# A two-layer decoder trunk: bias tables, value weights, score maxima and output splits moved in the order of work

## The chip, the cores and the metric

The kernel runs on one core of one Trainium2 chip. The metric is device time in microseconds for one execution of the whole program, the median of several runs. Five engines work side by side: TensorE (PE, with its weight loads shown as PEld), VectorE (DVE), ScalarE (ACT), GpSimd (POOL) and SyncE (SP), which here issues all transfers.

## The reference

Two decoder layers act on x of 512 rows by 1024 columns, in fp32. Each layer is: half-step SwiGLU feed-forward, token mixer, half-step SwiGLU feed-forward. Each of these six sub-layers is wrapped in the same way:

```
hn = rmsnorm(x, pre_g) * (1 + scale) + shift
y  = rmsnorm(fn(hn), post_g)
x  = x + res_w * gate * y          # shift, scale, gate from silu(c) @ w_mod + b_mod
ffn(h) = (silu(h @ w_gate) * (h @ w_up)) @ w_down            # inner width 2816
```

The mixer of layer 0 is latent attention with 16 heads. The mixer of layer 1, the one that the change touches, is dilated sliding-window attention with 16 heads of width 64 and three groups of dilation 1, 4 and 16:

```
proj = (h @ w_in)                  # per group g: queries, keys, values, 16 heads x 64
s    = q k^T / 8 + bias[bucket(rel * dilation)]    # -inf outside the window
lse  = logsumexp(s);  p = exp(s - lse);  o_g = p v
alpha = softmax over the three groups of lse
out  = (sum_g alpha_g o_g) @ w_o
```

The bias is a table of 32 buckets by 48 (16 heads for each of 3 groups), looked up by the bucketed distance. Since the groups are joined by a softmax over their log-sums, the kernel uses one maximum and one denominator over all three groups for each row and head.

## The kernel before

**Products.** Every fp32 weight tile is split into a high and a low half (`weights`, lines 128 to 136): a transfer into a "raw" buffer (5 of them), a copy on ScalarE that rounds to the high half (line 133), and two subtractions on VectorE, 512 columns each, for the low half (line 135). High and low halves live in rings of `SLOTS` = 6. A product is then three matrix multiplications, high by high, high by low and low by high (`mm3`, lines 148, 149 and 150). One projection tile is 8 such triples, 24 matrix multiplications of 128 by 512. Results go to PSUM banks under two tags, "mm" and "aux", with 4 banks each. SBUF tiles of 512 columns come from one pool of 44 slices; short-lived ones from small pools under the tags "silu", "gg" (2 buffers each), "sq" and "u" (4 each).

**Between sub-layers.** `transition` (line 478) finishes one sub-layer and starts the next: for each of four row blocks, the last products of the old one (`tail`), the norm and residual, transposes and modulation into the new h; after the second row block it calls the next sub-layer's `prepare`, and then its "heads", for the dilated layer six projection tiles of head pair 0, once for each half of the rows. Nothing here has an order written by hand: the planner orders by program order as priority and by its own idea of readiness.

**The dilated layer** (`Dil`, `rest` from line 1400). Heads are handled in 8 pairs. In `rest` the gates are fetched, the bias tables are made (`tables`: three one-hot tables of 33 by 384 and the bias table are loaded, three small products go to PSUM on line 989, are copied out and written to memory as `tv`), the bias tiles of pair 0 are read back from `tv` with a shifting row offset (`bias_of`, 12 transfers for a pair, line 1005), and then a loop with an order written by hand for TensorE, ScalarE and VectorE begins. In that loop, pair p attends while the projection tiles of pair p + 1 fill TensorE, six tiles (`ORDER`, slots n = 0 to 5), and for p = 0 and p = 4 twelve value tiles more (`value_tile`), which make the values of four or three pairs at once, group by group, four tiles each. SyncE and GpSimd are not part of the order by hand.

**A pair's start.** Slot n = 0 holds: transposes of the previous pair's group-0 probabilities on TensorE (`turn_up`, line 1244, two steps), their copies out of PSUM on VectorE (`turn_down`, line 1256), the scores of group 0 (`scores` 0 and 1, line 1118, two "mm" banks each), whose bias addition and row maximum is one VectorE instruction (line 1135), and the 32 by 32 transposes of group 2 on VectorE (line 1258). The projection tile of the slot follows. Slot 1 has the weighted sums of the previous pair (`weigh`, line 1277) and the scores of groups 1 and 2.

**Weights ahead.** `ahead` starts weight loads up to a given count beyond the tile at work. In the loop it keeps 5 tiles ahead; in the value tiles, up to 6, and in the last tile of each group of four one more load after each of the four pairs of row blocks (line 1345).

**The end of the layer.** After seven rounds the three value tiles of pair 7 are made (`LAST`); each tile's transposes to row order (line 1093) run behind the next tile, and the last one's as `later()`. Then each earlier pair's output is split into high and low (`put_o`, lines 711 and 712), the last pair's maxima go through memory to be joined across groups (`tops`), its exponentials follow (line 1194) and its denominators go through memory as well (`norm`, `norm_out`). Under a second order by hand, now for TensorE and VectorE alone, `part` n makes the output projection over the first `PART` = 3 pairs, eight parts, mixed with the last pair's turns and weighted sums. The other five pairs' products come in `tail`, in the next transition.

Of the kernel before, what the change touches and what calls it, by code (L numbers as in the profile page):

```python
# [22 lines left out]
PART = 3  # L23
# [3 lines left out]
SLOTS = 6  # L27
KQ = 2
UB = 4
SB = 4  # L30
# [506 lines left out]
class Ffn:  # L537
# [17 lines left out]
    def prepare(self):  # L555
        self.gate_up_load(0, True)
# [34 lines left out]
    def head(self, ft, lo, hi):  # L591
        banks = [self.t.bank()[:, : hi - lo] for g in range(2)]
        self.gate_up_mm(ft, lo, hi, banks, range(KT))
        self.gate_up_out(ft, lo, hi, banks)
# [371 lines left out]
class Dil(Mixer):  # L966
# [9 lines left out]
        (2, tuple((j, j * P, P, 384) for j in range(4))),  # L976
    )

    def tables(self):
        t, nc = self.t, self.t.nc  # L980
        self.tv = t.dram.tile([3, 16, 384], F32, name="tv")
        hot = [t.s() for _ in range(3)]
        tab = t.t("u", UB)
        nc.sync.dma_start(tab[0:32, 0:48], t.a["rel_bias"])
        nc.vector.memset(tab[32:33, 0:48], 1.0)
        for g in range(3):
            nc.sync.dma_start(hot[g][0:33, 0:384], t.a["dil_hot"][g])
            b = t.bank("aux")
            nc.tensor.matmul(
                b[0:16, 0:384], tab[0:33, 16 * g : 16 * g + 16], hot[g][0:33, 0:384], start=True, stop=True  # L990
            )
            v = t.t("gg")
            nc.vector.tensor_copy(v[0:16, 0:384], b[0:16, 0:384])
            nc.sync.dma_start(self.tv[g], v[0:16, 0:384])

# [47 lines left out]
    def head(self, u, lo, hi):  # L1043
        if lo == 0 and u == 0:
            self.qkv = {}
            self.pairs = {}
            self.later = None
        self.tile(0, self.ORDER[u], lo, hi)

    def prepare(self):  # L1050
        t = self.t
        self.wt = {(0, u): t.weights_sliced(t.a["dil_in"][0, u]) for u in self.ORDER[:2]}

    def tile(self, p, u, lo, hi):
        t, nc = self.t, self.t.nc
        g, kind = divmod(u, 3)
        n = hi - lo
        if lo == 0:
            if (p, u) not in self.wt:
                self.wt[p, u] = t.weights(t.a["dil_in"][p, u])  # L1060
            self.qkv[p, u] = t.s()
        w = self.wt[p, u]
        b = t.bank()[:, :n]
        for k in range(KT):
            t.mm3(b, [x[:, k, :] for x in w], [x[k][:, lo:hi] for x in t.h], k == 0, k == KT - 1)
        dst = self.qkv[p, u]
        runs = (SEQ, P, 32)[g]
        part = runs * n // SEQ
        at = runs * lo // SEQ
        if kind == 1:  # L1070
            at = runs - at - part
        for q in range(1 if g < 2 else 4):
            if g == 0:
                out, src = dst[:, at : at + part], b
            elif g == 1:
                out = dst.rearrange("p (r l) -> p r l", r=4)[:, :, at : at + part]
                src = self.order(b, 1)
            else:
                out = self.split(dst, 2)[:, q, :, at : at + part]
                src = self.order(b, 2)[:, q]  # L1080
            if kind == 1:
                src = self.back(src)
            nc.scalar.activation(out, src, AF.Copy)  # L1083
        turn, self.later = self.later, None
        if turn:
            turn()
        if kind == 2:

            def turn():
                x = t.bank("aux")  # L1090
                for j in range(4):
                    r = slice(j * P, (j + 1) * P)
                    nc.tensor.transpose(x[:, r], dst[:, r], t.ident)
                v = self.qkv[p, u] = t.s()
                nc.vector.tensor_copy(v, x)

            self.later = turn
# [232 lines left out]
    def value_tile(self, p, g, j):  # L1330

        t, nc = self.t, self.t.nc
        n = (self.BLOCKS_V[p][1] - p) * P
        if (g, j) == (0, 0):
            self.made = []
        if j == 0:
            wide = [t.wide() for _ in range(2)] if g < 2 else []
            halves = [x[:, d * SEQ : (d + 1) * SEQ] for x in wide for d in range(2)]
            self.made.append(halves or [t.s() for _ in range(4)])
        b = t.bank()[:, :n]  # L1340
        for k in range(KT):
            w = [x[:, k % 2 * n :][:, :n] for x in self.wt[p, g, k // 2]]
            h = [self.keys_of(x[k], g, j) for x in t.h]
            t.mm3(b, h, w, k == 0, k == KT - 1)
            if j == 3 and k % 2:
                self.ahead(self.at + SLOTS + k // 2 + 1)
        dst = self.made[g][j][:, :n]
        out = t.s()[:, :n] if g == 2 else dst
        nc.scalar.activation(out, b, AF.Copy)
        if g == 2:  # L1350
            for a in range(4):
                nc.sync.dma_start(
                    dst[32 * a : 32 * a + 32], out.rearrange("(l a) v -> a l v", a=4)[a]
                )
        if (g, j) == (2, 3):
            self.v = self.made

    def slot(self, p, n):

        if n == 0:  # L1360
            if p:
                up = [self.turn_up(p - 1, step) for step in range(2)]
                for step in range(2):
                    self.turn_down(p - 1, step, up[step])
            self.scores(p, 0)
            self.scores(p, 1)
            if p:
                self.turn(p - 1, 3)
        elif n == 1:
            if p == 7:  # L1370
                self.scores(p, 2)
                self.scores(p, 3, "aux")
            if p:
                for step in range(4):
                    self.weigh(p - 1, step)
            if p < 7:
                self.scores(p, 2)
                self.scores(p, 3, "aux")
        elif n == 4:
            self.biases(p + 1)  # L1380
        elif n == 5:
            self.turn(p, 2)
# [17 lines left out]
    def rest(self):  # L1400
        t = self.t
        t.gates(self)
        self.of = []
        self.bias = {}
        self.tables()
        self.biases(0)
        self.coming, self.loaded, self.at = self.loads(), 0, 0
        with t.tc.manual_schedule(engines={PE, ACT, DVE}):
            for p in range(7):
                values = [(p, g, j) for g in range(3) for j in range(4) if p in self.BLOCKS_V]  # L1410
                for n, at in enumerate([(p + 1, u) for u in self.ORDER] + values):
                    self.slot(p, n)
                    self.ahead(self.at + min(SLOTS - 1 + max(n - 6, 0) % 4, SLOTS))
                    self.beside(p, n)
                    if n < 6:
                        self.tile(*at, 0, SEQ)
                    else:
                        self.value_tile(*at)
                    self.behind(p, n)
                    if n < 6 or n % 4 == 1:  # L1420
                        self.at += 1 if n < 6 else 4
            for n, u in enumerate(self.LAST):
                self.slot(7, n)
                self.ahead(self.at + SLOTS - 1)
                self.beside(7, n)
                self.tile(7, u, 0, SEQ)
                self.at += 1
        self.later()
        for x in self.of[:PART]:
            self.put_o(x)  # L1430
        t.new_y()
        self.tops(self.pairs[7])
        for x in self.of[PART:]:
            self.put_o(x)
        for i in range(TT):
            t.unpark(i)
        self.exps(7, (2, 0, 1, 3))
        self.norm(self.pairs[7])
        order = (2, 0, 1, 3)
        with t.tc.manual_schedule(engines={PE, DVE}):  # L1440
            for n in range(6):
                self.part(n)
            for n, step in enumerate(order):
                self.turn(7, step)
                if n:
                    self.weigh(7, order[n - 1], order[0], order[-1])
                if n in (0, 1):
                    self.part(6 + n)
            self.norm_out(self.pairs[7])
            self.weigh(7, order[-1], order[0], order[-1])  # L1450
            self.finish(7)
        self.put_o(self.of[-1])
# [118 lines left out]
```

## Time and profile before

| | |
|---|---|
| median of 3 runs | 2277.46 us (2275.86 to 2278.70) |
| the profiled execution | 2277.86 us, span 2276.0 us |
| mean granted TensorE clock | 0.995 |
| TensorE busy | 2236.2 us, 98% |
| weight loads busy | 1879.6 us, 83% |
| VectorE busy | 1184.7 us, 52% |
| ScalarE busy | 849.8 us, 37% |
| GpSimd busy | 105.0 us, 5% |
| read from HBM | 281.76 MB, 126 GB/s over the span |

Reading: a timeline row gives start, duration, engine, line, operation, output and inputs, how many instructions were merged, and in square brackets the idle time of that engine before the row and what ended it. A row of a stage table gives the stretch, its length, for each of PE, PEld, DVE, ACT and POOL the busy time and the count, then the granted TensorE clock, the share of the transfer engines in use and the GB/s. A row of a group gives the line, engine, operation, tiles, shape, count, then busy time and mean ns of one, then idle time ahead of them and what ended most of it.

### The profile page before, as it was taken

What the parts mean: (1) busy time and instruction counts of PE and PEld (TensorE: products, weight loads), DVE (VectorE), ACT (ScalarE), POOL (GpSimd) and SP (SyncE); (2) the same over time, 40 slices, a digit from 0 to 9 for tenths busy, and PEclk for the clock granted to TensorE, in tenths of its full rate; (3) what the DMA queues carried; (4) which work ended last, traced back from release to release, by engine and by line L of the source; (5) the groups of instructions that cost most, each with busy time, mean ns of one, the idle gap of its engine ahead of it and who ended that gap; (6) DMA issues with size and microseconds to landing.
All of it is one profiled execution on the core that took longest, in us unless ns stands there. A gap on an engine that the chain in (4) does not pass through costs nothing.

```text
span 2276.0 us, 30275 instructions
## 1 busy us (share of the span) xinstructions
PE 2236.2 (98%) x11410; PEld 1879.6 (83%) x11410; DVE 1184.7 (52%) x2697; ACT 849.8 (37%) x1737; POOL 105.0 (5%) x143
## 2 busy tenths in 40 slices
PE   7999999999999999999999999999999999999998
PEld 5888888877888888898888887988898878888887
DVE  7666566577755456464555463234423457233344
ACT  4422235577623222353222353334342535332222
POOL 0000001210110000020000010000000002000000
PEclk9999999999999999999999999999999999999999
DMA  8575662211255365245544433433333442233231
GB/s 307 166 241 185 185 231 72 96 56 48 91 159 176 107 200 184 93 140 135 188 167 146 123 124 90 118 85 96 79 96 97 93 119 78 74 121 102 84 111 38
DMA packets 124344, 290.07 MB, mean 127 GB/s; under 512 B 44818, under 2 KB 49701, under 8 KB 124198
## 3 DMA queue, kind: packets, MB, share of 16 engines
q1 hardware_dynamic: 124198, 288.15, 41.1%
q8 instruction: 89, 1.46, 0.3%
q14 instruction: 57, 0.47, 0.1%
HBM read 281.76 MB, written 4.49 MB: 126 GB/s over the span
## 4 chain that ended last, share of the span: by engine, by line
PE 91%; DVE 3%; ACT 2%; issue 2%; POOL 1%; DMA 1%; POOLq 0%; DVEq 0%; SPq 0%; ACTq 0%
PE mm L148 28%; PE mm L149 28%; PE mm L150 28%; PE mm L880 1%; PE aux L1277 1%; PE mm L1118 1%; PE aux L929 1%; PE aux L1244 1%; POOL mv L323 1%; PE aux L908 1%; DVE wlo L135 1%; PE aux L528 1%; ACT whi L133 0%; DVE x L504 0%; PE aux L1118 0%
## 5 line engine op out<-in xcount | busy, mean ns | idle before, releaser
L135 DVE TENSOR_TENSOR wlo<-raw,whi 128x512 fp32r<-128x512 f32 (+2 forms) x718 | 467.6, 689 | 591.6 <-ACT whi L133 589.6
L148 PE MATMUL mm<-s,whi 128*128 128x512 f32 (+1 forms) x1948 | 730.4, 376 | 9.8 <-DVE dm L1135 7.3
L150 PE MATMUL mm<-s,wlo 128*128 128x512 f32 (+1 forms) x1948 | 726.2, 373 | 1.3 <-DVE wlo L135 1.3
L149 PE MATMUL mm<-s,whi 128*128 128x512 f32 (+1 forms) x1948 | 726.3, 373 | 0.0
L133 ACT ACTIVATE whi<-raw 128x1024 fp32r<-128x1024 f32 (+2 forms) x359 | 369.4, 1044 | 810.1 <-PE mm L149 548.1
L148 PEld LDWEIGHTS mm<-s,whi 128*128 128x128 f32 x1948 | 368.1, 189 | 78.8 <-issue 9.8
L150 PEld LDWEIGHTS mm<-s,wlo 128*128 128x128 f32 x1948 | 368.2, 189 | 66.3 <-DVE wlo L135 2.0
L149 PEld LDWEIGHTS mm<-s,whi 128*128 128x128 f32 x1948 | 368.7, 189 | 62.7
L148 PE MATMUL mm<-whi,s 128*128 128x512 f32 (+1 forms) x1040 | 406.9, 391 | 1.2 <-ACT s L711 1.2
L149 PE MATMUL mm<-wlo,s 128*128 128x512 f32 (+1 forms) x1040 | 405.1, 390 | 0.0
L150 PE MATMUL mm<-whi,s 128*128 128x512 f32 (+1 forms) x1040 | 404.7, 389 | 0.0
L148 PEld LDWEIGHTS mm<-whi,s 128*128 128x128 f32 x1040 | 212.4, 204 | 37.2 <-ACT s L711 1.8
L150 PEld LDWEIGHTS mm<-whi,s 128*128 128x128 f32 x1040 | 212.5, 204 | 35.1 <-DVE s L712 1.0
L149 PEld LDWEIGHTS mm<-wlo,s 128*128 128x128 f32 x1040 | 212.5, 204 | 34.2 <-issue 0.7
L170 DVE CUSTOM_DVE_ANT_0 raw<-raw,cs 128x1024 f32<-128x1024 f32 x130 | 160.6, 1240 | 122.3 <-DMA raw<-w_mod 122.1
L464 DVE TENSOR_TENSOR s<-mm,s 128x512 f32<-128x512 f32 x112 | 76.6, 689 | 118.9 <-PE mm L150 118.5
L323 POOL TENSOR_TENSOR mv<-mv,mhalf 128x1 f32<-128x1 f32 x48 | 36.2, 756 | 1503.8 <-DVE mv L322 1501.3
L1083 ACT ACTIVATE s<-mm 128x128 f32<-128x128 f32 (+3 forms) x114 | 34.4, 358 | 182.4 <-PE mm L150 178.5
L587 ACT ACTIVATE s<-gg 128x512 fp32r<-128x512 f32 (+1 forms) x97 | 57.4, 592 | 41.1 <-DVE gg L586 41.1
L586 DVE TENSOR_TENSOR gg<-silu,mm 128x512 f32<-128x512 f32 (+1 forms) x95 | 59.9, 630 | 10.5 <-ACT silu L584 10.5
L584 ACT ACTIVATE silu<-mm 128x512 f32<-128x512 f32 (+1 forms) x95 | 51.4, 541 | 17.5 <-PE mm L150 17.5
L149 PE MATMUL mm<-s 128*128 128x256 f32 (+1 forms) x176 | 53.2, 308 | 4.0 <-DVE s L312 3.1
(182 smaller groups left out, 1680.2 us busy)
## 6 DMA issues: line engine op xcount, KB each, us to landing
raw<-w_gu SPq DMA_DIRECT2D x168, 512.0 KB, 4.2
raw<-w_mod SPq DMA_DIRECT2D x130, 512.0 KB, 4.8
raw<-w_down SPq DMA_DIRECT2D x88, 512.0 KB, 4.5
raw<-dil_in SPq DMA_DIRECT2D x49, 512.0 KB, 5.0
s<-w_mod SPq DMA_DIRECT2D x28, 256.0 KB, 6.0
raw<-dil_v SPq DMA_DIRECT2D x12, 512.0 KB, 6.0
raw<-dil_v SPq DMA_DIRECT2D x12, 384.0 KB, 5.8
raw<-w_gu SPq DMA_DIRECT2D x16, 256.0 KB, 3.7
```

What stands on the lines that cost most here:

```text
L133: self.nc.scalar.activation(hi, raw, AF.Copy)
L135: self.nc.vector.tensor_tensor(lo[:, r], raw[:, r], f(hi[:, r]), ALU.subtract)
L148: mm(out, w[0], m[0], start=first, stop=False)
L149: mm(out, w[0], m[1], start=False, stop=False)
L150: mm(out, w[1], m[0], start=False, stop=last)
L170: nc.vector.tensor_tensor_reduce(raw, raw, self.cs, 1.0, 0.0, ALU.mult, ALU.add, accum_out=t[:, 0:1])
L323: nc.gpsimd.tensor_tensor(v[:, 1:2], v[:, 0:1], self.mhalf[:, 0:1], ALU.pow)
L464: nc.vector.tensor_tensor(y, b, y, ALU.add)
L584: nc.scalar.activation(s, banks[0], AF.Silu)
L586: nc.vector.tensor_tensor(v, s, banks[1], ALU.mult)
L587: nc.scalar.activation(ghi, v, AF.Copy)
L1083: nc.scalar.activation(out, src, AF.Copy)
```

## The change

There are four edits, all in the dilated layer.

1. The loads for the bias tables become a function `tables_in`, called at the end of `prepare`, into short-lived tiles instead of slices. The table products, copies and writes are called at the start of the first head, in the transition. In `rest`, four weight loads (`SLOTS` - 2) and then pair 0's bias reads are issued at the head of the order written by hand; the bias reads stood ahead of it.
2. In the last value tile of each group of four, `ahead` is called after the first two pairs of row blocks, not after all four; the two loads that fall away there are made by the calls of the next tiles.
3. In slot 0, the scores of block 0 and their maxima come ahead of the copies of the first turned step, and the scores of block 1 ahead of the copies of the second.
4. Six of the eight output splits move beside the second and third of the last value tiles, three each; the seventh follows `tops`. `part(0)` comes ahead of `later()`, which moves into the second order by hand.

```diff
+    def tables_in(self):
+        t, nc = self.t, self.t.nc
+        self.hot = [t.t(tag) for tag in ("silu", "silu", "gg")]
+        self.tab = t.t("sq", SB)
+        nc.sync.dma_start(self.tab[0:32, 0:48], t.a["rel_bias"])
+        nc.vector.memset(self.tab[32:33, 0:48], 1.0)
+        for g in range(3):
+            nc.sync.dma_start(self.hot[g][0:33, 0:384], t.a["dil_hot"][g])
+
     def tables(self):
         t, nc = self.t, self.t.nc
         self.tv = t.dram.tile([3, 16, 384], F32, name="tv")
-        hot = [t.s() for _ in range(3)]
-        tab = t.t("u", UB)
-        nc.sync.dma_start(tab[0:32, 0:48], t.a["rel_bias"])
-        nc.vector.memset(tab[32:33, 0:48], 1.0)
-        for g in range(3):
-            nc.sync.dma_start(hot[g][0:33, 0:384], t.a["dil_hot"][g])
+        for g, tag in enumerate(("gg", "silu", "silu")):
             b = t.bank("aux")
...
-            v = t.t("gg")
+            v = t.t(tag)
             nc.vector.tensor_copy(v[0:16, 0:384], b[0:16, 0:384])
             nc.sync.dma_start(self.tv[g], v[0:16, 0:384])
...
             self.later = None
+            self.tables()
         self.tile(0, self.ORDER[u], lo, hi)
...
         self.wt = {(0, u): t.weights_sliced(t.a["dil_in"][0, u]) for u in self.ORDER[:2]}
+        self.tables_in()
...
-            if j == 3 and k % 2:
+            if j == 3 and k in (1, 3):
                 self.ahead(self.at + SLOTS + k // 2 + 1)
...
                 up = [self.turn_up(p - 1, step) for step in range(2)]
-                for step in range(2):
-                    self.turn_down(p - 1, step, up[step])
             self.scores(p, 0)
+            if p:
+                self.turn_down(p - 1, 0, up[0])
             self.scores(p, 1)
             if p:
+                self.turn_down(p - 1, 1, up[1])
                 self.turn(p - 1, 3)
...
-        self.tables()
-        self.biases(0)
         self.coming, self.loaded, self.at = self.loads(), 0, 0
         with t.tc.manual_schedule(engines={PE, ACT, DVE}):
+            self.ahead(SLOTS - 2)
+            self.biases(0)
             for p in range(7):
...
                 self.ahead(self.at + SLOTS - 1)
+                if n:
+                    for x in self.of[n * 3 - 3 : n * 3]:
+                        self.put_o(x)
                 self.beside(7, n)
                 self.tile(7, u, 0, SEQ)
                 self.at += 1
-        self.later()
-        for x in self.of[:PART]:
-            self.put_o(x)
         t.new_y()
         self.tops(self.pairs[7])
-        for x in self.of[PART:]:
-            self.put_o(x)
+        self.put_o(self.of[-1])
...
         with t.tc.manual_schedule(engines={PE, DVE}):
-            for n in range(6):
+            self.part(0)
+            self.later()
+            for n in range(1, 6):
                 self.part(n)
```

More of the change, by code (lines that the diff above doesn't have):

```diff
@@ L981, in tables @@
         self.tv = t.dram.tile([3, 16, 384], F32, name="tv")
-        hot = [t.s() for _ in range(3)]
-        tab = t.t("u", UB)
-        nc.sync.dma_start(tab[0:32, 0:48], t.a["rel_bias"])
-        nc.vector.memset(tab[32:33, 0:48], 1.0)
-        for g in range(3):
-            nc.sync.dma_start(hot[g][0:33, 0:384], t.a["dil_hot"][g])
+        for g, tag in enumerate(("gg", "silu", "silu")):
             b = t.bank("aux")
             nc.tensor.matmul(
-                b[0:16, 0:384], tab[0:33, 16 * g : 16 * g + 16], hot[g][0:33, 0:384], start=True, stop=True
+                b[0:16, 0:384],
+                self.tab[0:33, 16 * g : 16 * g + 16],
+                self.hot[g][0:33, 0:384],
+                start=True,
+                stop=True,
             )
-            v = t.t("gg")
+            v = t.t(tag)
             nc.vector.tensor_copy(v[0:16, 0:384], b[0:16, 0:384])
```

## The prediction

> **What bounds the kernel now.** I read the page first, for the bound:
>
> ```profile
> span 2276.0 us, 30275 instructions
> PE 2236.2 (98%) x11410; PEld 1879.6 (83%) x11410; DVE 1184.7 (52%) x2697; ACT 849.8 (37%) x1737; POOL 105.0 (5%) x143
> L148 PE MATMUL mm<-s,whi 128*128 128x512 f32 (+1 forms) x1948 | 730.4, 376 | 9.8 <-DVE dm L1135 7.3
> ```
>
> TensorE is the bound nearly everywhere, and the change takes no matrix product away. What it can win is the time in which TensorE waits or runs at a lower clock in the dilated layer. The group of line 148 names the largest cause: 7.3 us on the score maxima (line 1135). So I went through TensorE's timeline of that layer and put each disturbed place beside an undisturbed one of the same work.
>
> Timeline of TensorE: the start of pair 0 (A), of pair 1 (B), of pair 2 (undisturbed), of pair 5 (C), and the end of the last projection (D).
>
> ```profile
> 1378.58 2.10 PE L989 MATMUL aux<-s,u 33*16 33x384 f32 x6
> 1380.61 1.79 PE L1118 MATMUL mm<-s 64*128 64x128 f32 x16
> 1385.57 0.77 PE L148 MATMUL mm<-s,whi 128*128 128x512 f32 x1 [3.17 <-DVE dm L1135]
> 1388.02 0.80 PE L150 MATMUL mm<-s,wlo 128*128 128x512 f32 x1 [1.25 <-DVE wlo L135]
> 1394.86 1.16 PE L1118 MATMUL mm<-s 64*128 64x128 f32 x16
> ...
> 1493.58 1.79 PE L1118 MATMUL mm<-s 64*128 64x128 f32 x16
> 1497.42 0.47 PE L148 MATMUL mm<-s,whi 128*128 128x512 f32 x1 [2.05 <-DVE dm L1135]
> 1503.08 1.08 PE L1277 MATMUL aux<-silu,x 128*64 128x256 f32 x8
> ...
> 1538.35 1.79 PE L1118 MATMUL mm<-s 64*128 64x128 f32 x16
> 1545.93 1.08 PE L1277 MATMUL aux<-silu,x 128*64 128x256 f32 x8
> ...
> 1728.32 1.79 PE L1118 MATMUL mm<-s 64*128 64x128 f32 x16
> 1732.16 0.47 PE L148 MATMUL mm<-s,whi 128*128 128x512 f32 x1 [2.05 <-DVE dm L1135]
> 1739.39 1.08 PE L1277 MATMUL aux<-silu,x 128*64 128x256 f32 x8
> ...
> 1841.97 0.60 PE L1093 MATMUL aux<-ident,s 128*128 128x128 f32 x4
> 1843.27 0.83 PE L1093 MATMUL aux<-ident,s 128*128 128x128 f32 x4 [0.69 <-ACT s L1083]
> 1845.25 0.57 PE L148 MATMUL mm<-whi,s 128*128 128x512 f32 x1 [1.15 <-ACT s L711]
> 1849.18 0.39 PE L148 MATMUL mm<-whi,s 128*128 128x512 f32 x1
> ```
>
> The same 16 score products and one projection tile (24 products) take 1545.93 - 1538.35 = 7.58 us undisturbed, but 14.25 us in A (1394.86 - 1380.61), 9.50 in B and 11.07 in C. The waits alone do not explain A and C; the granted clock does the rest:
>
> ```profile
> 1378.50:1394.90 16.40, 11.98 (x50) 7.61 (x48) 10.24 (x29) 0.57 (x4) 0.00 (x0) 0.79 0.28 56
> 1493.50:1503.10 9.60, 7.55 (x44) 5.75 (x42) 6.93 (x24) 0.25 (x1) 0.00 (x0) 1.00 0.64 189
> 1538.30:1546.00 7.70, 7.56 (x44) 5.80 (x44) 6.16 (x23) 3.41 (x15) 0.00 (x0) 1.00 0.41 114
> 1728.30:1739.40 11.10, 9.05 (x43) 6.91 (x42) 6.86 (x24) 0.08 (x1) 0.20 (x1) 0.85 0.47 155
> ```
>
> The third number from the end is the clock: 0.79 in A and 0.85 in C, full in B and in pair 2.
>
> **Part 1, bias tables made in the transition (A).** Now the one-hot tables are fetched early but multiplied only after the last head product, and the bias of pair 0 makes a trip through memory after that.
>
> ```profile
> 1288.62 9.88 SPq L65 DMA_DIRECT2D raw<-dil_in  x4
> ...
> 1340.64 0.28 PE L148 MATMUL mm<-s 128*128 128x256 f32 x1
> 1344.29 0.39 PE L148 MATMUL mm<-s 128*128 128x256 f32 x1 [0.43 <-ACT s L311]
> ...
> 1356.84 1.10 SPq L987 DMA_DIRECT2D s<-dil_hot  x3
> ...
> 1361.00:1378.50 17.50, 17.50 (x148) 17.44 (x146) 0.00 (x0) 5.51 (x15) 0.00 (x0) 1.00 0.01 2
> 1369.93 1.06 ACT L133 ACTIVATE whi<-raw 128x1024 fp32r<-128x1024 f32 x1 [2.38 <-PE mm L149]
> 1372.81 1.06 ACT L133 ACTIVATE whi<-raw 128x1024 fp32r<-128x1024 f32 x1 [1.55 <-PE mm L149]
> ...
> 1379.43 1.19 DVE L993 COPY gg<-aux 16x384 f32<-16x384 f32 x2 [20.96 <-PE aux L989]
> ...
> 1381.53 0.82 SPq L1005 DMA_DIRECT2D s<-tv  x2
> ...
> 1384.78 0.29 DVE L1135 CUSTOM_DVE_ANT_0 sq<-mm,s 128x128 f32<-128x128 f32 x1 [2.63 <-DMA s<-tv]
> ```
>
> The chain is products 1378.58, copies 1379.43, bias reads from 1381.53, first maximum 1384.78. Scores fill all four "mm" banks, so the tile behind them needs the first maxima. With the products moved to 1340.64, the first head product, the same chain of 1384.78 - 1378.58 = 6.2 us ends near 1347; even with all twelve bias reads queued behind the weight fetches it has until 1380. The second wait in A (1.25, low halves of the first tile's weights) goes because four loads now stand ahead of the first scores in VectorE's order: the high halves of two of them wait until head units 2 and 3 give up their slots (line 133 at 1369.93 and 1372.81), and the window 1361.00:1378.50 has VectorE 0.00 busy for the eight subtractions. That empty window is the cover; without it they would delay the maxima by 8 halves. The 2.10 us of table products only change place. A falls from 14.25 to 7.58: **6.67 us**.
>
> Not shown before: the table products amid the modulation. Three copies of 1.19/2 = 0.6 us join a busy VectorE (cost at most 1.8 if all land on the path), while 2.1 us of work at 1340.64 gives the modulation time to get ahead and may swallow waits such as the 0.43 at 1344.29 (gain at most about 1.0, were there two such). I take 0, since the copies stand behind the first modulation in program order.
>
> **Parts 2 and 3, two weight loads fewer per value group, and maxima ahead of turned copies (B, C).**
>
> ```profile
> 1489.08 5.52 DVE L135 TENSOR_TENSOR wlo<-raw,whi 128x512 fp32r<-128x512 f32 x8 [17.03 <-ACT whi L133]
> 1494.51 1.28 DVE L1256 COPY silu<-aux 128x512 f32<-128x512 f32 x2
> ```
>
> Four loads come in the last value tile, eight halves of 0.69 us; the turned copies start only behind them at 1494.51 and the maxima behind those copies, so the tile waits until 1497.42. With two loads VectorE is free 4 x 0.69 = 2.8 us earlier, near 1491.8, before the scores of 1493.58; and the first maxima no longer stand behind the copies. Either edit nearly does it; together B and C fall to 7.58: **1.92 and 3.49 us**. The other pair starts have no wait, and gain nothing. What is queued later: the turned copies now stand behind a wait for the scores, and the weighted sum (line 1277) wants them one tile later; that tile (5.66 us from 1497.42 to 1503.08) covers the 2.8 us by which they can slip. The two deferred loads are asked for four tiles later, 4 x 5.66 = 22.6 us of cover; cost 0.
>
> [...]
>
> **Part 4, outputs split beside the last values (D).** TensorE waits for the copy of the last value tile, held up on ScalarE, then for the first split output, and then runs slow until 1849.18. From 1841.97 that is 7.21 us for 8 transposes and 9 products. Undisturbed: two fours of 0.60 and 9 x 5.66/24 = 2.1, together 3.3. With six outputs split one and two tiles earlier, and the first part between the two groups of transposes as cover for that copy (2.1 us against 0.69 waited), D gives **3.9 us**. Six splits move into the fixed order of ScalarE and VectorE. Three stand before the previous pair's denominators, so that pair's last multiplication slips by up to 3 x 0.69 = 2.1 us; behind it wait the copies that free banks, which have four "mm" banks of slack. I take 0; the ends are 0 and 2.1 lost.
>
> **The sum.** 6.67 + 1.92 + 3.49 + 3.9 = 16.0. Ends of the unknown costs: 16.0 + 1.0 = 17.0 and 16.0 - 1.8 - 2.1 = 12.1. The profiled execution took 2277.86 (span 2276.0 and 1.9 around it); minus 16.0 is 2261.9. It lies 0.4 above the median of the runs shown, so against the median 2261.5; the ends give 2260.5 to 2265.4. Behind D TensorE stays the bound, so nothing later gives the gain back, save the first rival.
>
> **Rivals.** (1) The end holds. The last pair's output is needed just when it is ready:
>
> ```profile
> 1869.79 0.14 DVE L1218 TENSOR_TENSOR w<-x 128x8 f32<-128x8 f32 x1
> ...
> 1880.62 0.69 DVE L1297 TENSOR_TENSOR s<-aux,s 128x512 f32<-128x512 f32 x1 [7.55 <-DMA s<-d]
> 1882.01 0.69 DVE L712 TENSOR_TENSOR s<-s 128x512 fp32r<-128x512 f32 x1 [0.70 <-ACT s L711]
> ...
> 1882.10 0.42 PE L148 MATMUL mm<-whi,s 128*128 128x512 f32 x1
> ```
>
> If that chain of two trips through memory (1869.79 to 1882.70) does not move with TensorE, D's 3.9 come back as a wait there: 2265.4. For it: no slack at 1882.10. Against: its start is tied to the turned copies of the last pair, which TensorE itself releases. (2) Pair 0's bias still late, since its reads queue on SP behind weight fetches that wait for buffers: A stays, 2268.2. For it: SP issues in order. Against: 40 us of room. That the planner leaves the table products at their old place ends in the same time. (3) Slower. TensorE's order takes the table products to 1340.64, but their fetch keeps its place on SP (issued until 1357.94); with the 3.25 us that a bias read took (1381.53 to 1384.78) TensorE would stand from 1340.64 to 1361.2, 20.6 us: 2261.5 + 20.6 = 2282.1. It decides once the fetch lands over 16 us after the first head product. For it: that is where SP has it now. Against: the fetch is issued with the weights of the same function, and those went out at 1288.62. (4) Little happens, because the planner shuffles the free parts of the transition: about 2275.
>
> **Chances.** Forecast 0.72, (1) 0.12, (2) 0.08, (3) 0.04, (4) 0.04. I take 0.2% (4.6 us) as what a measurement can tell from no change. Faster: the forecast, (1) and (2), 0.92, less 0.02 for several small losses at once: 0.90; same 0.05; slower 0.05. The range 2257 to 2269 holds the forecast with its ends, (1) and (2), and some gain from the transition that I did not count.
>
> **What would show it.** Right: no wait of line 148 on line 1135 anywhere, a clock of 1.00 at the starts of pairs 0, 1 and 5 and 7.6 us for each, table products near 1340, and part 0 directly behind four transposes. Wrong: a new wait on the table products, on the last split output near the tail, or on the low halves in a value group; a tail of unchanged length with D gone would show rival 1.

## The result, and the profile after

The changed kernel takes 2259.11 us (median of 4 runs, 2258.32 to 2259.99), the kernel before 2277.93 beside it (4 runs, 2275.86 to 2278.70): a ratio of 0.9919, with a 95% interval from 0.9902 to 0.9936. I had forecast 2261.5, with a range from 2257 to 2269. The gain is 18.8 us by the medians; I had forecast 16.0.

The page of the profile after, and the group of line 148 on it (all lines of the dilated layer lie about 10 further down than before: the maxima are now line 1145, the scores 1128, the turned copies 1266, the weighted sums 1287, the table products 993, the transposes of the end 1103):

```profile
span 2256.5 us, 30280 instructions
PE 2226.5 (99%) x11410; PEld 1874.1 (83%) x11410; DVE 1183.5 (52%) x2697; ACT 849.1 (38%) x1737; POOL 107.2 (5%) x143
L148 PE MATMUL mm<-s,whi 128*128 128x512 f32 (+1 forms) x1948 | 728.0, 374 | 2.7 <-ACT whi L133 2.3
```

The 7.3 us on the maxima are gone from the group; what is left, 2.3 us on ScalarE's weight copy, is a wait at the start of the program. The timeline of TensorE after, at the same five places as in the prediction (A, B, the undisturbed pair 2, C, D):

```profile
1378.85 1.86 PE L1128 MATMUL mm<-s 64*128 64x128 f32 x16
1386.32 1.16 PE L1128 MATMUL mm<-s 64*128 64x128 f32 x16
...
1485.05 1.79 PE L1128 MATMUL mm<-s 64*128 64x128 f32 x16
1492.43 1.08 PE L1287 MATMUL aux<-silu,x 128*64 128x256 f32 x8
...
1527.71 1.79 PE L1128 MATMUL mm<-s 64*128 64x128 f32 x16
1535.11 1.08 PE L1287 MATMUL aux<-silu,x 128*64 128x256 f32 x8
...
1717.16 1.79 PE L1128 MATMUL mm<-s 64*128 64x128 f32 x16
1724.55 1.08 PE L1287 MATMUL aux<-silu,x 128*64 128x256 f32 x8
...
1826.79 0.60 PE L1103 MATMUL aux<-ident,s 128*128 128x128 f32 x4
1827.14 0.48 PE L148 MATMUL mm<-whi,s 128*128 128x512 f32 x1
1829.31 0.60 PE L1103 MATMUL aux<-ident,s 128*128 128x128 f32 x4
1829.66 0.49 PE L148 MATMUL mm<-whi,s 128*128 128x512 f32 x1
```

Read as differences of starts: A 1386.32 - 1378.85 = 7.47, B 7.38, pair 2 7.40, C 7.39, D 1829.66 - 1826.79 = 2.87. TensorE's timeline has no wait in any of these stretches. The stage table of A, B and C (columns as in the prediction; the clock is the third number from the end) shows TensorE busy throughout and no slow stretch left:

```profile
1378.80:1386.40 7.60, 7.60 (x44) 5.94 (x42) 3.79 (x18) 0.57 (x4) 0.00 (x0) 1.00 0.18 18
1485.00:1492.50 7.50, 7.50 (x44) 5.79 (x44) 6.50 (x24) 0.17 (x1) 0.00 (x0) 1.00 0.34 99
1717.10:1724.60 7.50, 7.50 (x44) 5.78 (x43) 6.48 (x24) 0.08 (x1) 0.20 (x1) 1.00 0.37 103
```

Not all of the profiled difference belongs to the change. TensorE's timeline has the first transposes of the transition into the dilated layer at this place, first before, then after:

```profile
1331.40 1.80 PE L528 MATMUL aux<-ident,s 128*128 128x128 f32 x15
```

```profile
1329.87 1.91 PE L528 MATMUL aux<-ident,s 128*128 128x128 f32 x16
```

All that the change touches on TensorE lies behind this row, and it already stands 1.53 us earlier. From it to the end of the span are 2276.0 - 1331.40 = 944.6 us before and 2256.5 - 1329.87 = 926.6 after: the change is worth 18.0 us, and 1.5 of the profiled 19.5 came from elsewhere (last section). How much of such a part is in the medians' 18.8 is not shown, since only one execution of each kernel was profiled. I use this distance, from the first transposes to the end, for all kernels below.

| place | before | after | gain | predicted |
|---|---|---|---|---|
| transition, first transposes to first scores | 49.21 | 48.98 | 0.23 | 0 |
| A, start of pair 0 | 14.25 | 7.47 | 6.78 | 6.67 |
| B, start of pair 1 | 9.50 | 7.38 | 2.12 | 1.92 |
| C, start of pair 5 | 11.07 | 7.39 | 3.68 | 3.49 |
| starts of pairs 2, 3, 4, 6, 7, each | 7.58 | 7.40 | 5 x 0.18 | 0 |
| D, end of the last projection | 7.21 | 2.87 | 4.34 | 3.9 |
| sum | | | 18.05 | 15.98 |

The sum of the places is the distance's 18.0, so nothing was given back behind D.

### The profile page after: what moved, and what is told of

Its sections match the earlier page's. It is cut to its first block, busy times and chain, and to the rows that moved or that the text cites. A ratio compares the mean times of both kernels' runs of the same rounds, so it can differ in the third digit from the quotient of the medians.

```text
span 2256.5 us, 30280 instructions
## 1 busy us (share of the span) xinstructions
PE 2226.5 (99%) x11410; PEld 1874.1 (83%) x11410; DVE 1183.5 (52%) x2697; ACT 849.1 (38%) x1737; POOL 107.2 (5%) x143
## 3 DMA queue, kind: packets, MB, share of 16 engines
q8 instruction: 89, 1.46, 0.3%
## 4 chain that ended last, share of the span: by engine, by line
PE 93%; ACT 2%; DVE 2%; issue 2%; POOL 1%; DMA 0%; POOLq 0%; DVEq 0%; ACTq 0%
PE mm L148 28%; PE mm L149 28%; PE mm L150 28%; PE aux L1287 1%; PE mm L880 1%; PE mm L1128 1%; PE aux L1254 1%; PE aux L929 1%; POOL mv L323 1%; PE aux L908 1%; PE aux L528 0%; ACT whi L133 0%; DVE x L504 0%; PE aux L1128 0%; DVE wlo L135 0%
```

## The experiments

Each part was first put alone into the kernel before; then two parts were split in two, two parts were taken out of the whole, and two kernels went after what the result showed upstream. The table gathers what TensorE's timeline says for each. A is from the first scores of pair 0 to the next; B and C are here from the first scores of pairs 1 and 5 to the next scores, which is 10.98 at an undisturbed start of before and 10.80 after; D is as above; "rest" is the distance from the first transposes to the end of the span. Each ratio is to the kernel before as timed beside that kernel (medians of 2277.93 for the whole change, 2278.30 for the single parts and 2279.45 for the two kernels that leave one part out and the two that go upstream). Four kernels ran once, for their trace: their times carry no verdict.

| kernel | median us (runs) | ratio, 95% interval | A | B | C | D | rest |
|---|---|---|---|---|---|---|---|
| before | 2277.93 (4) | 1 | 14.25 | 12.91 | 14.48 | 7.21 | 944.6 |
| tables alone | 2271.57 (7) | 0.9973 [0.9962, 0.9983] | 7.47 | 14.51 | 14.49 | 7.22 | 939.2 |
| loads alone | 2273.05 (11) | 0.9976 [0.9967, 0.9984] | 14.67 | 11.00 | 10.99 | 8.50 | 941.4 |
| order alone | 2271.44 (9) | 0.9971 [0.9962, 0.9981] | 14.72 | 10.79 | 10.79 | 7.61 | 938.8 |
| splits alone | 2273.62 (11) | 0.9981 [0.9972, 0.9990] | 14.64 | 14.48 | 12.89 | 2.87 | 940.8 |
| tables, no loads ahead | 2274.59 (1) | | 9.40 | 14.49 | 14.47 | 8.13 | 942.9 |
| loads ahead, tables late | 2277.21 (1) | | 12.06 | 12.90 | 14.49 | 7.24 | 942.7 |
| splits early, copy first | 2275.55 (1) | | 14.58 | 14.54 | 12.88 | 3.33 | 941.0 |
| part 0 first, splits late | 2277.55 (1) | | 14.87 | 14.48 | 14.49 | 6.21 | 945.8 |
| whole without loads | 2261.37 (5) | 0.9915 [0.9901, 0.9928] | 7.47 | 10.80 | 10.79 | 2.88 | 926.7 |
| whole without order | 2261.23 (4) | 0.9918 [0.9905, 0.9932] | 7.47 | 11.00 | 10.96 | 2.88 | 928.0 |
| whole change | 2259.11 (4) | 0.9919 [0.9902, 0.9936] | 7.47 | 10.79 | 10.80 | 2.87 | 926.6 |
| whole, second value tile moved | 2258.81 (4) | 0.9909 [0.9895, 0.9922] | 7.47 | 10.80 | 10.79 | 2.88 | 926.7 |
| whole, fourth value tile moved | 2257.70 (4) | 0.9905 [0.9891, 0.9918] | 7.47 | 10.79 | 10.79 | 2.88 | 926.7 |

(B and C without the parts for them jump between 12.9 and 14.5, with the same wait of 2.05 us: see the last section.)

### The four parts alone

The tables' part alone: one-hot tables fetched in `prepare`, multiplied ahead of the heads, and four loads ahead of the loop.

```diff
+        self.tables_in()
...
+            self.tables()
         self.tile(0, self.ORDER[u], lo, hi)
...
-        self.tables()
-        self.biases(0)
...
+            self.ahead(SLOTS - 2)
+            self.biases(0)
```

> The first edit alone: table products in the transition, four weight loads and the bias reads at the head of the order by hand; all else as before. Theory (each place is won by its own edit): the start of pair 0 (scores to the next scores) falls from 14.25 us to about 7.5, clock there 1.00, the starts of pairs 1 and 5 stay at 9.5 and about 11 with their 2.05 us waits, the end D stays at 7.2; total 6.8 us faster, ratio 0.997. Rival (the gain is lost in the transition, where the copies of the tables delay the modulation): the start of pair 0 falls the same but the first half of the heads takes up to 1.8 us longer, total about 5.

The loads' part alone:

```diff
-            if j == 3 and k % 2:
+            if j == 3 and k in (1, 3):
```

> The second edit alone: two weight loads instead of four in the last value tile of a group. Theory (either of edits 2 and 3 does nearly all of it): VectorE is free 2.8 us earlier, the starts of pairs 1 and 5 fall from 9.50 and 11.07 us to about 7.6, as pair 2 has it, total 5.4 us faster, ratio 0.9976; pair 2 stays at 7.58. Rival (the order of the copies is what counts): a wait of line 148 on line 1135 of 1 us or more is left in pairs 1 and 5.

The order's part alone:

```diff
             if p:
                 up = [self.turn_up(p - 1, step) for step in range(2)]
-                for step in range(2):
-                    self.turn_down(p - 1, step, up[step])
             self.scores(p, 0)
+            if p:
+                self.turn_down(p - 1, 0, up[0])
             self.scores(p, 1)
             if p:
+                self.turn_down(p - 1, 1, up[1])
                 self.turn(p - 1, 3)
```

> The third edit alone: first maxima ahead of the turned copies. Theory (either does it): the eight halves end at the same time as before, the maxima follow at once, the starts of pairs 1 and 5 fall to about 7.5, and the other five starts, which showed no wait, to 7.40 from 7.58; total 5.4 + 5 x 0.18 = 6.3 us faster, ratio 0.9972. Rival (the eight halves are what counts): pairs 1 and 5 keep a wait of 1 us or more, total 1 us or less beside the five starts.

The splits' part alone:

```diff
+                if n:
+                    for x in self.of[n * 3 - 3 : n * 3]:
+                        self.put_o(x)
...
-        self.later()
...
+            self.part(0)
+            self.later()
+            for n in range(1, 6):
```

> The fourth edit alone: six output splits beside the last value tiles, part 0 ahead of the last transposes. Theory: the end D (from the second four transposes to the part after the third four) falls from 7.21 us to about 2.9, total 4.3 us faster, ratio 0.998. Rival (the end holds): D falls the same, but the products with the last pair's output wait up to 4 us on lines 711 or 712 near the tail, total 0 to 1.

By their medians against the 2278.30 of before (27 runs beside them), the parts gain 6.7, 5.3, 6.9 and 4.7 us. All four add up to 23.6, more than the whole change's 18.8; tables, order and splits alone add up to 18.3. So loads and order gain the same thing. Each takes the wait at B and at C away by itself, which its trace shows. The splits alone have D at 2.87, as in the whole. One thing was not foreseen: the loads alone have a longer D, 8.50, because their first split output comes later (a wait of 2.38 us on it instead of 1.15). ScalarE's timeline there shows what holds it:

```profile
1841.27 0.40 ACT L1194 ACTIVATE sq<-sq,y 128x128 f32<-128x128 f32 x1 [1.20 <-DMA y<-t]
```

The first split copy (line 711, at 1842.17) stands on ScalarE behind two exponentials of the last pair, and these wait for that pair's joined maxima to come back from memory (y<-t). In the six kernels that lack the splits' part, ScalarE stands there for 0 (before), 0.16, 0.28, 0.33, 0.72 and 1.20 us, and TensorE's wait for the first split is 1.15, 1.34, 1.46, 1.50, 1.89 and 2.38 us, in the same order: always about 1.18 more. So the late first split is a trip through memory that ends late. The longer D is not tied to the loads' part: the tables moved without loads ahead, whose value tiles load as before, have 8.13. In this trace it takes 1.3 us from the loads' gain. The 7.21 of before is the lowest D of the six, so the splits may be worth more than 4.34 us in other executions. What sets the length of that trip was not tested.

### The tables' part in two

The tables moved, but no loads ahead of the first scores:

```diff
-            self.ahead(SLOTS - 2)
             self.biases(0)
```

> The first edit without its four weight loads at the head of the order by hand: tables in the transition, bias reads early, weight loads behind the first maxima as before. Theory (two separate causes in the start of pair 0): the wait on line 1135 is gone, the wait for the low halves stays and grows to about 2.0 us, since ten halves still stand behind eight maxima; the start of pair 0 takes 9.5 us at full clock or 11.1 at the lower one, against 14.25 before and 7.5 with the whole edit. Rival (the low halves were late only because the maxima were): 7.5, no wait.

The loads ahead, with the tables at their old place:

```diff
+            self.ahead(SLOTS - 2)
+            self.biases(0)
```

> The other half of the first edit: four weight loads ahead of the first scores, tables at their old place. Theory: the 3.2 us wait on the bias stays, the 1.25 us wait on the low halves goes, the clock still falls; the start of pair 0 takes about 13.0 us. Rival (the loads do most of it): under 10.

TensorE's timeline at pair 0, first for the tables without the loads ahead, then for the loads ahead without the tables:

```profile
1378.92 1.86 PE L1128 MATMUL mm<-s 64*128 64x128 f32 x16
1383.11 0.50 PE L150 MATMUL mm<-s,wlo 128*128 128x512 f32 x1 [1.67 <-DVE wlo L135]
1388.32 0.94 PE L1128 MATMUL mm<-s 64*128 64x128 f32 x12
```

```profile
1381.87 1.79 PE L1118 MATMUL mm<-s 64*128 64x128 f32 x16
1386.71 0.47 PE L148 MATMUL mm<-s,whi 128*128 128x512 f32 x1 [3.06 <-DVE dm L1135]
1393.93 1.16 PE L1118 MATMUL mm<-s 64*128 64x128 f32 x16
```

Each half takes away one of the two waits and leaves the other. With the tables moved the wait on the maxima goes and 9.40 us are left; the loads then take off 9.40 - 7.47 = 1.93 us more. The loads by themselves bring A to 12.06, 0.9 less than I expected, since the slow stretch is shorter too, in this one execution: a clock of 0.86 over 12.2 us here, 0.79 over 16.4 us before.

### The splits' part in two

The six splits early, but the last value tile's second copy still ahead of the parts:

```diff
+                if n:
+                    for x in self.of[n * 3 - 3 : n * 3]:
+                        self.put_o(x)
...
         self.later()
-        for x in self.of[:PART]:
-            self.put_o(x)
```

> The fourth edit without its change of order: six splits early, but the last four transposes still ahead of part 0. Theory (the late split and the lower clock behind it are the cost, the order of part 0 saves the 0.7 us wait for the last copy): from the second four transposes to the end of part 0 it takes about 3.8 us, against 7.2 before and 2.9 with the whole edit. Rival (part 0 ahead is what counts): over 6.

The first part ahead of that copy, but the splits late:

```diff
-        self.later()
...
+            self.part(0)
+            self.later()
+            for n in range(1, 6):
```

> The other half of the fourth edit: part 0 ahead of the last transposes, splits at their old place. Theory: part 0 waits about 3 us for the first split on line 711 and then runs at the lower clock; from the second four transposes to the end of both about 7.0 us, a gain of 0.3 or none. Rival: the gain is 3 us or more.

TensorE's timeline at D, the four transposes and what follows, first with the splits early, then with part 0 first:

```profile
1843.61 0.60 PE L1093 MATMUL aux<-ident,s 128*128 128x128 f32 x4
1843.97 0.48 PE L148 MATMUL mm<-whi,s 128*128 128x512 f32 x1
...
1844.52 0.40 PE L150 MATMUL mm<-whi,s 128*128 128x512 f32 x1
1845.00 0.49 PE L1093 MATMUL aux<-ident,s 128*128 128x128 f32 x2
...
1846.94 0.39 PE L148 MATMUL mm<-whi,s 128*128 128x512 f32 x1
```

```profile
1842.65 0.60 PE L1093 MATMUL aux<-ident,s 128*128 128x128 f32 x4
1844.96 0.50 PE L148 MATMUL mm<-whi,s 128*128 128x512 f32 x1 [1.71 <-ACT s L711]
1846.53 0.50 PE L148 MATMUL mm<-whi,s 128*128 128x512 f32 x1 [0.19 <-ACT s L711]
1848.86 0.49 PE L148 MATMUL mm<-whi,s 128*128 128x512 f32 x1
```

With the splits early D is 1846.94 - 1843.61 = 3.33 us, though the copy is written first: the planner itself filled three of part 0's products into the wait for it. Counted in this order, and against the 7.21 of before, the early splits are worth 7.21 - 3.33 = 3.9 of the 4.34 us, and writing part 0 first the other 0.5. With the splits late, part 0 first has nothing ready to multiply and D stays at 6.21, a gain of 1.0, where I expected 0.3 or none.

### Loads or order taken out of the whole

The whole change, with four loads per last value tile again:

```diff
-            if j == 3 and k in (1, 3):
+            if j == 3 and k % 2:
```

> The whole change, with one part undone: the last value tile of a group asks for four weight loads again (k odd) instead of two; the maxima stay ahead of the turned copies. The full reference is computed. Theory (either of the two edits is enough at a pair's start): no wait of TensorE on the maxima at the starts of pairs 1 and 5, 16 score products and one tile take 7.40 us there as in the whole change, and the time is that of the whole change, 2259 us, ratio 0.992 with 0.001 either way. Rival (the low halves of four loads end late enough that the maxima, though first, come late with the other parts in place): a wait of 1 us or more comes back at pair 1 or 5 or both, ratio 0.993 or above.

The whole change, with all turned copies ahead of the scores again:

```diff
+                for step in range(2):
+                    self.turn_down(p - 1, step, up[step])
             self.scores(p, 0)
-            if p:
-                self.turn_down(p - 1, 0, up[0])
             self.scores(p, 1)
             if p:
-                self.turn_down(p - 1, 1, up[1])
                 self.turn(p - 1, 3)
```

> The whole change, with one part undone: at a pair's start all turned copies stand ahead of the scores again, as before; two loads per last value tile stay. The full reference is computed. Theory (the loads alone take the wait away at pairs 1 and 5, and the moved maxima give only the small gain at each of the seven pair starts): no wait on the maxima, 7.58 us instead of 7.40 from the scores to the end of the next tile at the undisturbed pairs, seven times 0.18 = 1.3 us slower than the whole change, 2260.4 us, ratio 0.9925. Rival (the order is what takes the wait away once the other parts are in place): waits of about 2 us on the maxima come back at pairs 1 and 5, ratio 0.994.

VectorE's timeline at the start of pair 1, first without the loads' part, then without the order's part:

```profile
1483.49 5.52 DVE L135 TENSOR_TENSOR wlo<-raw,whi 128x512 fp32r<-128x512 f32 x8 [17.03 <-ACT whi L133]
1488.95 0.29 DVE L1145 CUSTOM_DVE_ANT_0 sq<-mm,s 128x128 f32<-128x128 f32 x1
```

```profile
1482.20 2.71 DVE L135 TENSOR_TENSOR wlo<-raw,whi 128x512 fp32r<-128x512 f32 x4 [10.96 <-ACT whi L133]
1485.72 1.29 DVE L1266 COPY silu<-aux 128x512 f32<-128x512 f32 x2 [0.81 <-PE aux L1254]
1486.92 1.01 DVE L1266 COPY gg<-aux 128x384 f32<-128x384 f32 x2
1487.85 0.28 DVE L1145 CUSTOM_DVE_ANT_0 sq<-mm,s 128x128 f32<-128x128 f32 x1
```

In the first, eight halves end as the first maximum starts, 0.96 us behind the scores at 1487.99. In the whole change it is 0.95 (1486.00 behind 1485.05), so the halves have no slack left but cost nothing. In the second, the four halves are long done; the copies hold the first maximum until 1.15 us behind the scores at 1486.70, and the tile starts 0.18 us late. Distances to the end agree: 926.7 without the loads, as for the whole; 928.0 without the order, 1.4 more, which is 7 x 0.18 and a rest of 0.1. The medians of these two kernels (2261.37 and 2261.23) can't tell them apart; the first one's runs go from 2258.46 to 2262.26.

### More cover upstream

The whole change, and in the latent attention of layer 0 the second value tile behind the first query:

```diff
         self.value(0, 0)
-        self.value(1, 0)
         self.key(0, 1)
         self.t.count(99)
         self.rope(0)
         self.query(0, 0)
+        self.value(1, 0)
         self.value(2, 0)
```

> The whole change, and one step of the attention before the dilated layer moved: the second value tile behind the first query instead of ahead of the second key, so that a tile of matrix products lies over the two waits (0.64 and 0.78 us near 448 us) after which the granted clock falls to about 0.86 for some 10 us in part of the runs. The full reference is computed. Theory (those waits and the clock behind them cost 1.4 us by themselves and about as much again when the clock falls): 1.4 to 2.9 us faster than the whole change, 2256.2 to 2257.7 us, ratio 0.9905 to 0.991. Rival (what the tile covered where it stood opens instead): a wait on the norms of the key appears earlier, the time is within 1 us of the whole change or above it, ratio 0.992 or more.

The whole change, and the fourth value tile of that attention made ahead of its first block instead of beside the third:

```diff
-        2: (("value", 3, 0),),
...
         self.value(2, 0)
+        self.value(3, 0)
```

> The whole change, and one step of the attention before the dilated layer moved: the fourth value tile goes from beside the third block of that attention to ahead of it, behind the third value tile, as more cover for the two waits near 448 us. The full reference is computed. Theory (cover is what these waits lack): they go, no fall of the clock behind them, 1.4 to 2.9 us faster than the whole change, ratio 0.9905 to 0.991. Rival (the tile is missed where it stood, or stands too late to cover the waits): the waits stay at 0.64 and 0.78, or a new one of like size appears some 40 us later; time within 1 us of the whole change or above it, ratio 0.992 or more.

TensorE's timeline where the first block's scores begin, first of the whole change, then with the second value tile moved, then with the fourth:

```profile
447.88 0.49 PE L880 MATMUL mm<-s 96*128 96x128 f32 x2 [0.64 <-ACT s L837]
449.15 1.35 PE L880 MATMUL mm<-s 96*128 96x128 f32 x6 [0.78 <-ACT s L820]
```

```profile
440.82 0.74 PE L148 MATMUL mm<-s,whi 128*128 128x512 f32 x2 [0.32 <-ACT s L777]
...
448.34 0.49 PE L880 MATMUL mm<-s 96*128 96x128 f32 x2 [0.41 <-ACT s L837]
449.61 1.35 PE L880 MATMUL mm<-s 96*128 96x128 f32 x6 [0.78 <-ACT s L820]
```

```profile
448.58 0.38 PE L879 MATMUL mm<-s 96*128 96x128 f32 x2
449.30 1.81 PE L879 MATMUL mm<-s 96*128 96x128 f32 x6 [0.34 <-ACT s L820]
```

Moving the second tile opens the wait that it had covered (0.32 us at 440.82), as the rival said. Its four runs, 2258.67 to 2258.85, are no gain over the whole change. Moving the fourth takes the first wait away and leaves 0.34 us of the second; the first transposes come at 1329.15, 0.72 earlier than in the whole change, and the rest is the same (926.65). Its four runs take 2257.65 to 2258.27, median 2257.70, ratio 0.9905 [0.9891, 0.9918]. That is the lowest time of all, 1.4 us under the whole change's median, at the lower edge of what I expected, but the intervals of the two ratios overlap, and the two were not timed side by side. The trace shows 0.7 us by itself.

## Why the prediction was right, and where it was off

**Part 1 (A): right, and for the reason given.** Predicted 6.67, measured 6.78. The table products stand ahead of the heads (line 993, from 1339.20), and everything behind them had room. SyncE's timeline after shows the chain:

```profile
1342.23 0.32 SPq L1002 DMA_DIRECT2D tv<-gg  x1
...
1346.36 0.35 SPq L1002 DMA_DIRECT2D tv<-silu  x1
1347.66 6.08 SPq L125 DMA_DIRECT2D raw<-dil_in  x5
...
1359.99 6.59 SPq L1013 DMA_DIRECT2D s<-tv  x12
```

The twelve bias reads do queue behind the weight fetches, as rival (2) had it (they start at 1359.99, behind a fetch that waited 5.7 us for line 135 and went out at 1359.57), but go out by 1366.6, 13 us ahead of the first maximum at 1379.81. "I take 0" for the table products amid the modulation was a fair middle: the transition gained 0.23 us, and the waits of 0.43 and 0.19 us became one of 0.62.

**Parts 2 and 3 (B, C): the mechanism right, one sentence wrong.** "Either edit nearly does it" was too weak for the wait of 2.05 us: either edit takes it away whole. B is 11.00 with the loads alone and 10.79 with the order alone; the 0.2 between them is the next point. The wrong sentence is "the other pair starts have no wait, and gain nothing". Pair 2's own stage row in the prediction has TensorE busy for 7.56 of 7.70 us, and the gap lies where the first tile waits for a bank that the maxima free: the scores end at 1538.35 + 1.79 = 1540.14, the tile starts at 1540.28, and VectorE starts the first maxima only at 1539.50, behind the turned copies. The trace puts no wait on this gap of 0.14 us. With the maxima first, each of seven starts gains 0.18 us, 1.3 in all, of which B and C are 0.2 each. The kernel without the order's part shows it: 10.98 instead of 10.80 at every start, and 1.4 us more in all. The turned copies slipped, and nobody waited for them.

The size of C's term was partly luck. Of its 3.49 us, 1.6 are lower clock (0.85 at C), which the same wait of 2.05 us at B did not have (1.00) in the execution that I read. In the six other kernels that keep both waits, the lower clock came after 9 of 12 of them, at B as well as at C (about 14.5 us from scores to scores instead of 12.9; last section). With a fall at both places or at neither, the same working would have given 1.6 us more or less.

The term also counts on a full clock once the wait is gone. The trace after shows it: C has a clock of 1.00 and no wait, behind 14 transposes (line 1254, 1.69 us from 1715.55).

**Part 4 (D): right, with one term mis-sized.** I took "two fours of 0.60". That is the duration of a merged row: the one at 1826.79 ends at 1827.39, 0.25 us after the start of the next row at 1827.14. From start to start a four takes 1827.14 - 1826.79 = 0.35 us. Two of them and part 0 are 0.35 + 2.17 + 0.35 = 2.87, not 3.3. The gain was 4.34, not 3.9. The prediction did not say what made the first split late; it is the trip of the last pair's maxima (see the four parts alone), and with six splits ahead of it the wait goes all the same.

**What did not happen.** Rival (1) said that the end holds. VectorE's timeline after shows the chain of the last pair moved with TensorE:

```profile
1850.40 0.13 DVE L1228 TENSOR_TENSOR w<-x 128x8 f32<-128x8 f32 x1
...
1860.43 0.69 DVE L1307 TENSOR_TENSOR s<-aux,s 128x512 f32<-128x512 f32 x1 [6.75 <-DMA s<-d]
1861.82 0.69 DVE L712 TENSOR_TENSOR s<-s 128x512 fp32r<-128x512 f32 x1 [0.70 <-ACT s L711]
```

It starts 19.39 us earlier (1850.40 against 1869.79) and its last row starts 20.19 earlier (1861.82 against 1882.01), because its start hangs on copies that TensorE releases, as the prediction argued against the rival. Rival (3) did not come: the fetches of the one-hot tables went out from 1298.35 on. Nor did rival (4). The 2.1 us by which the last multiplication of the previous pair could slip were used in part (it stands at 1829.32, with a wait of 1.41 us for its own transfer) and cost nothing.

So the prediction was 2.4 us too high by the medians: 0.9 + 0.4 from pair starts that I had written off, 0.4 from D, 0.3 from A and the transition, together 2.1 in the profile. The 1.5 us upstream are no part of the change and were in no step of it.

## What to carry to other kernels

Where a tile waits for a bank, put whatever frees the bank ahead of other work on that engine. This paid a little even where the trace shows no wait (0.18 us at a pair's start here); compare busy time with the length of the stretch. When one wait has two causes in a row, each edit alone may gain all of it: the sum of single gains (23.6 here against 18.8) shows what is counted twice. Don't put work that is ready early behind work on the same engine that waits for a trip through memory, as the splits stood behind the exponentials here. Size a group of matrix products by the distance of starts, not by the duration of its row.

## What the runs showed of the hardware

The granted clock fell after waits of 2.05 us, of 0.95 us and of 0.64 and 0.78 us one after the other, in some executions and not in others. Stage tables: the start of pair 1 before, then the same stretch with the tables' part alone, each with one wait of 2.05 us:

```profile
1493.58:1506.49 12.91, 10.86 (x90) 8.54 (x89) 6.85 (x24) 0.77 (x2) 0.00 (x0) 1.00 0.46 139
```

```profile
1486.60:1501.11 14.51, 12.46 (x90) 9.66 (x89) 6.84 (x24) 0.77 (x2) 0.00 (x0) 0.88 0.43 123
```

The same 90 products and the same wait take 1.60 us more in the execution in which the clock fell (14.51 us at a mean of 0.88, against 12.91 at 1.00). Of the 14 such waits at B and C in the profiled executions of seven kernels, 10 were followed by the fall and 4 were not. The same happens upstream, in code that only the last two kernels change. Before, two steps of 2 us behind the waits of 0.64 and 0.78 us:

```profile
450.00:452.00 2.00, 2.00 (x6) 1.54 (x6) 0.98 (x5) 1.99 (x6) 0.19 (x1) 0.50 0.28 109
452.00:454.00 2.00, 2.00 (x9) 1.58 (x8) 0.33 (x2) 1.13 (x5) 0.00 (x0) 0.78 0.00 0
```

The clock is 0.87 from 448 to 450, then 0.50 and 0.78 in these rows, and 1.00 from 454 on: the lost 0.26, 1.00 and 0.44 us add up to 1.70. Over 450 to 460 us its mean is 0.86 before and 1.00 after. The scores ahead of it start 0.06 us earlier before than after (447.82 and 447.88), the transposes behind it 1.57 us later (460.87 and 459.30): this is the 1.53 us of the result's section. Nine of the twelve profiled executions with these two waits have the fall. After a wait of 0.95 us near 403 us it came in 4 of 14 (over 400 to 410 us the mean clock is 0.83 with the loads' part alone and in the whole without that part, 1.00 before and after). With neither, one or both, the first transposes of the transition lie near 1329.9, 1331.4 and 1332.7. That the scatter between the runs of one kernel is made of the same steps is argued, not shown, since only one execution of each was profiled; nor did I find what decides whether the clock falls.
